# Seven products in the second phase of a feed-forward network, and products that collect on PSUM banks

## The chip, the cores and the metric

The kernel runs on one core of one Trainium2 chip. The metric is the device time of one execution in microseconds. Lower is better.

## What is computed

The reference is one layer of a streaming encoder over 1024 prompt frames and 64 sample frames (T = 1088 tokens) of width 1024. Two feed-forward networks stand around an attention and a convolution branch. The change touches the two feed-forward networks alone:

```
def _swiglu(x, g, w_in, w_out):
    a, b = jnp.split(_rms(x, g) @ w_in, 2, axis=-1)
    return (jax.nn.silu(a) * b) @ w_out

h = x + 0.5 * _swiglu(x, ffn1_norm, ffn1_w_in, ffn1_w_out)
...
h = h + 0.5 * _swiglu(h, ffn2_norm, ffn2_w_in, ffn2_w_out)
```

`w_in` is 1024 x 5632 and `w_out` is 2816 x 1024. The 2816 features are 22 tiles of 128. All values are fp32.

## The kernel before

**Precision.** Each fp32 operand is split into two parts in the type fp32r: `hi` is a copy on ACT, `lo = x - hi` a subtraction on DVE or POOL (`split`, lines 148 to 152). A product of two operands is three matmuls, hi x hi, hi x lo and lo x hi (`mm3`, lines 133 to 137), all into the same PSUM bank.

**Tokens and calls.** h lies in SBUF with channels on the partitions: 8 channel tiles by 1088 tokens, in four token quarters of `HW` = 272. `ffn` is called four times: for each of the two networks once for each half of the tokens (s = 0 or 1), and a half is two quarters c = 0 and 1. A call goes through its 22 feature tiles in groups (`GROUPS`, sizes 4, 4, 4, 3, 3, 4). Each group has a phase 1, which makes the group's features g, and a phase 2, which multiplies g by the group's rows of `w_out` and adds half of the result to h.

**Phase 1** (`wops`, `product`, `up`) makes one feature tile for both quarters. Its gate and linear columns, two halves of the channels and two token quarters form a 2 x 2 by 2 x 2 block product, which Strassen's method (in Winograd's form) computes with seven block products instead of eight. `prep` makes the seven operands of the tokens once for a call (`xop`). `wops` loads the two weight blocks of the tile (512 KB each, issued on SP's queue into `raw`) and makes the seven operands of the weights: `halves` splits the first block as it is, four sums `s` are formed on DVE, and `put` splits them and the block b1 into tiles `wp`. Sums 0 and 2 lie in PSUM banks, 1 and 3 in SBUF tiles. A product is 4 x 3 = 12 matmuls. Each of the seven goes to a fresh PSUM bank, and `up` adds it on DVE to sums held in SBUF (`spare`, `u3`). Silu and multiplication follow, and a split of g into `gh` and `gl`.

**Phase 2** (`part`, `ph2`) is a plain product. For each of the 16 pairs (dm, c) of a channel tile and a quarter, the G feature tiles of the group are accumulated on one bank, G x 3 matmuls, and line 427 adds half of the bank to h on DVE. Weights come in four blocks of two channel tiles, each split as a whole (`wload`, ACT then POOL). The first `NOPEN` = 3 pairs are opened with G - 1 tiles each, so that PE has work while the last tile of phase 1 is finished.

**Order of the work.** The program is written for a tile framework that puts the instructions of each engine in one static order, by a simulated timeline and by priorities; `high_priority(n)` moves a block's instructions n places ahead. `WAHEAD` = 4000 is that of all weight loading and preparation. Each engine runs its instructions in that order. Buffers are few: eight PSUM banks for everything in these stages, three `raw` buffers (`NRAW`), six `wp` tiles (`NPART`), four `s` tiles, three pairs `whi`, `wlo`, and four pairs `gh`, `gl`. A buffer's next writer waits for its last reader. Normalisation of other tokens (`stats`, `prep`, `apply`) is put between, one step after each feature tile and one after every second pair of phase 2, from the generator `steps`; in the last group of a call the function `tail` does so.

In the first call, the first two products of three feature tiles in each of the first two groups (`LEAD`) are computed ahead, while the second quarter of the tokens is being normalised.

Of the kernel before, what the change touches and what calls it, by code (L numbers as in the profile page):

```python
# [9 lines left out]
F32 = mybir.dt.float32  # L10
F32R = mybir.dt.float32r
# [4 lines left out]
AF = mybir.ActivationFunctionType  # L16
ALU = mybir.AluOpType
AX = mybir.AxisListType

P = 128  # L20
D = 1024
KT = 8
# [7 lines left out]
HW = 272  # L30
GROUPS = [4, 4, 4, 3, 3, 4]
LEAD = (3, 3)
NRAW = 3
AHEAD, LAG = 2, 2
# [57 lines left out]
class Kern:  # L92
# [40 lines left out]
    def mm3(self, out, wh, wl, xh, xl, first, last):  # L133
        t = self.nc.tensor
        t.matmul(out, wh, xh, start=first, stop=False)  # L135
        t.matmul(out, wh, xl, start=False, stop=False)  # L136
        t.matmul(out, wl, xh, start=False, stop=last)  # L137
# [151 lines left out]
    def wops(self, offs, a11=True):  # L289

        nc = self.nc
        res = [None] * 7
        with self.tc.high_priority(WAHEAD):
            ra, rb = (self.wraw.tile([P, 1024], F32, name="raw", tag="raw") for _ in range(2))
            for t, o in ((ra, offs[0]), (rb, offs[1])):
                nc.sync.dma_start(t, self.a["wf"][o:o + P * 1024].rearrange("(p n) -> p n", p=P))
            if a11:
                res[0], res[1] = self.halves(ra)
            a0, a1, b0, b1 = ra[:, 0:512], ra[:, 512:1024], rb[:, 0:512], rb[:, 512:1024]
            s = [self.wsum.tile([P, 512], F32, name="s", tag="s") if i % 2 else self.psum() for i in range(4)]  # L300
# [6 lines left out]
            nc.vector.tensor_tensor(s[0], b0, b1, op=ALU.add)  # L307
            nc.vector.tensor_tensor(s[1], s[0], a0, op=ALU.subtract)
            put(2, s[1])
            put(4, s[0])  # L310
            nc.vector.tensor_tensor(s[2], a0, b0, op=ALU.subtract)
            put(3, s[2])
            nc.vector.tensor_tensor(s[3], a1, s[1], op=ALU.subtract)
# [26 lines left out]
    def up(self, w, gp, tp, lead=None):  # L340
        nc = self.nc
        v = nc.vector.tensor_tensor
        self.turn ^= 4
        p1, sa, u2, c22 = (self.spare[:, self.turn + i, :] for i in range(4))
        u3 = tp.tile([P, HW], F32, name="u3", tag="u3", bufs=2)
        if lead:
            p1, sa = lead
        else:
            self.up1(w[0], w[1], p1, sa)
        v(u2, p1, self.product(w[2], 2), op=ALU.add)  # L350
        v(u3, u2, self.product(w[3], 3), op=ALU.add)
        p5 = self.product(w[4], 4)
        v(u2, u2, p5, op=ALU.add)
        v(c22, u3, p5, op=ALU.add)
        g = gp.tile([P, 2 * HW], F32R, name="gh", tag="gh"), gp.tile([P, 2 * HW], F32R, name="gl", tag="gl")
        c = self.product(w[5], 5)
        v(c, u3, c, op=ALU.add)
        v(c, sa, c, op=ALU.mult)
        self.split(g[0][:, :HW], g[1][:, :HW], c)
        c = self.product(w[6], 6)  # L360
        v(c, u2, c, op=ALU.add)
        nc.scalar.activation(c, c, AF.Silu)
        v(c, c22, c, op=ALU.mult)
        self.split(g[0][:, HW:], g[1][:, HW:], c)
        return g

    def ffn_offs(self):
        return [([(self.woff(), self.woff()) for _ in range(G)], [self.woff(2 * G * P) for _ in range(4)])
                for G in GROUPS]

    def ffn(self, h, s, offs, gp, tp, steps, tail, lead=(), ready=(), last=False, lp=None):
# [4 lines left out]
        for gi, n in enumerate(lead):  # L376
            for j in range(n):
# [5 lines left out]
                t = lp.tile([P, 2 * HW], F32, name="gl", tag="gl") if gi else \  # L383
                    gp.tile([P, 2 * HW], F32, name="gf", tag="gh")
                early[gi, j] = t[:, :HW], t[:, HW:]
                self.up1(*w, *early[gi, j])
                next(steps, None)
        if lead:
            run(ready)
        for gi, (wi, wo) in enumerate(offs):  # L390
            G = len(wi)
            gs = []
            for j in range(G):
                e = early.get((gi, j))
                gs.append(self.up(self.wops(wi[j], e is None), gp, tp, e))
                next(steps, None)
            per = 2
            wu = {}

            def part(dm, c, p, js):  # L400
                wh, wl = wu[dm // per]
                b = slice(c * HW, c * HW + HW)
                for j in js:
                    o = ((dm % per) * G + j) * P
                    self.mm3(p, wh[:, o:o + P], wl[:, o:o + P], gs[j][0][:, b], gs[j][1][:, b], j == 0, j == G - 1)

            def ph2(tiles, n, then):

                ps = {}
                for i, (dm, c) in enumerate(tiles):  # L410
                    if dm // per not in wu:
                        wu[dm // per] = self.wload(wo[dm // per], per * G * P)
                    if i < n:
                        if i == 0:
                            for q in tiles[:n]:
                                if q[0] // per not in wu:
                                    wu[q[0] // per] = self.wload(wo[q[0] // per], per * G * P)
# [12 lines left out]
            if gi < len(offs) - 1 or not last:  # L430
                ph2([(dm, c) for dm in range(KT) for c in (0, 1)], NOPEN,
                    (lambda dm, c: c and next(steps, None)) if gi < len(offs) - 1 else tail)
# [6 lines left out]
    def run(self):  # L439
        tc, nc, a = self.tc, self.nc, self.a  # L440
        PS = bass.MemoryType.PSUM
        with ExitStack() as top:
# [59 lines left out]
            gp = self.pool(ffw, "gp1", 4)  # L502
# [880 lines left out]
            gp = self.pool(top, "gp2", 4, side="right")  # L1383
# [45 lines left out]
def _pack_ffn(out, w1, w2):  # L1429
    j0 = 0  # L1430
    for G in GROUPS:
# [3 lines left out]
        for u in range(4):  # L1435
            blk = w2[j0 * P:(j0 + G) * P, u * 2 * P:(u + 1) * 2 * P].reshape(G, P, 2, P)
            out.append(blk.transpose(1, 2, 0, 3).ravel())
# [107 lines left out]
```

## Time and profile before

| | |
|---|---|
| median of three runs | 2393.53 us (2390.45 to 2393.75) |
| the profiled execution | 2389.32 us, span 2387.5 us |
| PE busy | 2291.5 us, 96%, 16610 matmuls |
| DVE busy | 1658.5 us, 69% |
| POOL busy | 1418.2 us, 59% |
| ACT busy | 1197.3 us, 50% |
| granted clock of PE, mean | 0.984 |
| DMA | 273.42 MB, mean 115 GB/s |

PE is TensorE, DVE VectorE, ACT ScalarE, POOL GpSimd, SP SyncE. In a row of a group of instructions stand the line, the engine, the operation, out<-in by the program's names, the shapes, the count, then the busy time in us and the mean of one in ns, and then the idle time of the engine just before them with what ended it. Matmuls are pipelined, so the mean of one is longer than the distance from one to the next. In a row of the waits view stand the waiting engine and line, what it waited for, the sum in us, how often, and the longest.

### The profile page before, as it was taken

Reading aid. Unit: us, or ns where it says so; the run is one execution under the profiler, and the core shown is the slowest. Engines: PE = TensorE matmul, PEld = TensorE weight load, DVE = VectorE, ACT = ScalarE, POOL = GpSimd, SP = SyncE. Lnnn points to the kernel's source line nnn. Section 1 sums busy time; section 2 is a strip of 40 time slices with the busy share of each in tenths; the row PEclk is TensorE's granted clock in tenths of the full one; section 3 lists DMA queues with packets and bytes.
Section 4 is the critical chain, followed back from the end, with each engine's and each line's share of the span. In section 5 each row is a group of like instructions: output and inputs, shape, how many; then the busy total and the mean of one; then the engine's idle time right before and its main releaser. Section 6 shows DMA issues by size and latency. Waiting matters only on the chain. (4 is left out here: it accounts for less than half of the span.)

```text
span 2387.5 us, 43966 instructions
## 1 busy us (share of the span) xinstructions
PE 2291.5 (96%) x16610; PEld 2262.8 (95%) x16610; DVE 1658.5 (69%) x3722; ACT 1197.3 (50%) x2286; POOL 1418.2 (59%) x879
## 2 busy tenths in 40 slices
PE   6999999999999999999979899899999999999998
PEld 6999999999999999999979789799999999999997
DVE  7766677767668387689846777358766678676666
ACT  6343444434345546887556667445433445434343
POOL 5455555555557786888953555467455555455554
PEclk9999999999999999999989999999999999999999
DMA  5323233233223344234222455763222331332223
GB/s 193 106 96 103 92 98 109 99 106 105 82 98 122 129 146 120 90 106 128 95 83 76 141 165 180 222 197 127 79 98 90 106 101 65 119 108 98 89 98 117
DMA packets 130406, 273.42 MB, mean 115 GB/s; under 512 B 17936, under 2 KB 77200, under 8 KB 130192
## 3 DMA queue, kind: packets, MB, share of 16 engines
q1 hardware_dynamic: 130192, 270.61, 35.1%
q8 instruction: 130, 2.13, 0.4%
q14 instruction: 84, 0.69, 0.1%
HBM read 231.87 MB, written 38.75 MB: 113 GB/s over the span
## 5 line engine op out<-in xcount | busy, mean ns | idle before, releaser
L118 POOL TENSOR_TENSOR wlo<-raw,whi 128x1024 fp32r<-128x1024 f32 (+1 forms) x187 | 433.8, 2325 | 356.1 <-ACT whi L117 345.3
L135 PE MATMUL ps<-x,wp 128*128 128x272 f32 x1760 | 506.9, 290 | 2.9 <-ACT wp L151 2.9
L137 PE MATMUL ps<-x,wp 128*128 128x272 f32 x1760 | 504.2, 290 | 1.4 <-DVE wp L152 1.0
L136 PE MATMUL ps<-x,wp 128*128 128x272 f32 x1760 | 505.3, 288 | 0.0
L135 PE MATMUL ps<-x,whi 128*128 128x272 f32 (+2 forms) x1544 | 482.5, 313 | 9.8 <-DVE sg L622 3.2
L137 PE MATMUL ps<-x,wlo 128*128 128x272 f32 (+2 forms) x1544 | 481.2, 312 | 0.0
L136 PE MATMUL ps<-x,whi 128*128 128x272 f32 (+2 forms) x1334 | 412.3, 309 | 0.9 <-POOL x L152 0.9
L135 PE MATMUL ps<-gh,whi 128*128 128x272 f32 x1408 | 400.6, 290 | 5.6 <-DVE spare L283 3.9
L136 PE MATMUL ps<-gl,whi 128*128 128x272 f32 x1408 | 405.6, 290 | 0.0
L137 PE MATMUL ps<-gh,wlo 128*128 128x272 f32 x1408 | 404.6, 289 | 0.0
L152 POOL TENSOR_TENSOR wlo<-raw,whi 128x1024 fp32r<-128x1024 f32 x88 | 220.1, 2502 | 259.3 <-ACT whi L151 248.3
L135 PEld LDWEIGHTS ps<-x,wp 128*128 128x128 f32 x1760 | 331.7, 188 | 4.0 <-ACT wp L151 3.8
L137 PEld LDWEIGHTS ps<-x,wp 128*128 128x128 f32 x1760 | 329.2, 188 | 3.1 <-DVE wp L152 2.5
L136 PEld LDWEIGHTS ps<-x,wp 128*128 128x128 f32 x1760 | 332.0, 189 | 0.0
L152 POOL TENSOR_TENSOR wp<-s,wp 128x512 fp32r<-128x512 f32 x176 | 256.5, 1457 | 98.1 <-ACT wp L151 98.1
L135 PEld LDWEIGHTS ps<-x,whi 128*128 128x128 f32 x1544 | 293.0, 190 | 12.2 <-DVE sg L622 3.5
L117 ACT ACTIVATE whi<-raw 128x1024 fp32r<-128x1024 f32 (+1 forms) x187 | 190.3, 1019 | 211.7 <-DMA raw<-wf 97.2
L137 PEld LDWEIGHTS ps<-x,wlo 128*128 128x128 f32 x1544 | 292.9, 190 | 1.3
L427 DVE SCALAR_TENSOR_TENSOR h<-ps,h 128x272 f32<-128x272 f32 x384 | 164.9, 439 | 185.7 <-PE ps L137 185.0
L679 POOL TENSOR_TENSOR ac<-ac,pd 128x559 f32<-128x559 f32 x180 | 270.5, 1503 | 39.2 <-ACT pd L678 13.7
L135 PEld LDWEIGHTS ps<-gh,whi 128*128 128x128 f32 x1408 | 263.7, 189 | 7.2 <-DVE spare L283 4.5
L137 PEld LDWEIGHTS ps<-gh,wlo 128*128 128x128 f32 x1408 | 266.6, 190 | 0.0
(254 smaller groups left out, 4818.6 us busy)
## 6 DMA issues: line engine op xcount, KB each, us to landing
raw<-wf SPq DMA_DIRECT2D x337, 512.0 KB, 3.4
raw<-wf SPq DMA_DIRECT2D x32, 384.0 KB, 3.2
d_g<-sg SPq DMA_DIRECT2D x32, 181.0 KB, 1.9
d_h<-h SPq DMA_DIRECT2D x2, 2176.0 KB, 10.7
y<-t SPq DMA_DIRECT2D x32, 136.0 KB, 1.9
raw<-d_q SPq DMA_DIRECT2D x32, 128.0 KB, 3.5
raw<-d_qi SPq DMA_DIRECT2D x24, 128.0 KB, 3.1
d_g<-sg SPq DMA_DIRECT2D x16, 182.0 KB, 3.3
```

The source lines that it names most:

```text
L117: nc.scalar.activation(hi[:, :n], raw[:, :n], AF.Copy)
L118: self.weng.tensor_tensor(lo[:, :n], raw[:, :n], hi[:, :n], op=ALU.subtract)
L135: t.matmul(out, wh, xh, start=first, stop=False)
L136: t.matmul(out, wh, xl, start=False, stop=False)
L137: t.matmul(out, wl, xh, start=False, stop=last)
L152: (eng or nc.vector).tensor_tensor(lo, x, hi, op=ALU.subtract)
L427: nc.vector.scalar_tensor_tensor(x, p, 0.5, x, op0=ALU.mult, op1=ALU.add)
L679: nc.gpsimd.tensor_tensor(ac, ac, pd, op=ALU.add)
```

## The change

Five things change together.

- `GROUPS` becomes 4, 4, 4, 4, 2, 4.
- Phase 2 of a group of four that is not the last of its call (`down`) also becomes a 2 x 2 by 2 x 2 block product with seven products: over the even and the odd tile of a pair of feature tiles, the lower and the upper half of the channels, and two token quarters. `up` makes the seven operands of g for a pair (t1 to t4 are their sums), in tiles of seven planes. `wops` makes those of the weights. `down` is called twice for a group (u = 0 and 1), each time for two channel tiles (i) of each half. Groups of two and the last group keep the plain phase 2, with the weights packed in another order.
- Products collect on banks. In `up`, products 2 and 3 are accumulated onto the bank of product 0, product 6 onto that of 4, and 5 onto that of 0, 2 and 3; between them `keep` copies the bank's state to SBUF on ACT, at priority `CHI` = 8000, or DVE reads it. In `down`, the banks "a" (products 0, 2, 3, 5) and "d" (4, 6) work alike, and after each product DVE adds the bank to the quarter and half of h that it belongs to; product 1 has bank "b".
- The order of the products becomes 0, 4, 2, 1, 3, 6, 5.
- In `wops`, ACT first copies b0 to a PSUM bank, so that three of the four sums have one operand there. With `sb` (in `down`), the other three sums lie in SBUF, and POOL makes every `lo` but that of sum 0, which DVE makes. `halves` copies its block in two pieces.

The core of the diff (the code that makes the weights' packing and the plain phase 2 is left out):

```diff
-GROUPS = [4, 4, 4, 3, 3, 4]
+GROUPS = [4, 4, 4, 4, 2, 4]
+CHI = 8000
...
-    def wops(self, offs, a11=True):
+    def wops(self, offs, a11=True, sb=False):
 
         nc = self.nc
         res = [None] * 7
+        v = nc.vector.tensor_tensor
         with self.tc.high_priority(WAHEAD):
             ra, rb = (self.wraw.tile([P, 1024], F32, name="raw", tag="raw") for _ in range(2))
             for t, o in ((ra, offs[0]), (rb, offs[1])):
@@ -297,38 +299,47 @@
             if a11:
                 res[0], res[1] = self.halves(ra)
             a0, a1, b0, b1 = ra[:, 0:512], ra[:, 512:1024], rb[:, 0:512], rb[:, 512:1024]
-            s = [self.wsum.tile([P, 512], F32, name="s", tag="s") if i % 2 else self.psum() for i in range(4)]
-
-            def put(o, x):
+            s = [self.wsum.tile([P, 512], F32, name="s", tag="s") if i % 2 or (sb and i) else self.psum()
+                 for i in range(4)]
+
+            def put(o, x, eng=None):
                 t = self.wpart.tile([P, 1024], F32R, name="wp", tag="wp")
                 res[o] = t[:, 0:512], t[:, 512:1024]
-                self.split(*res[o], x, nc.vector if o in (3, 4) else self.weng)
-
-            nc.vector.tensor_tensor(s[0], b0, b1, op=ALU.add)
-            nc.vector.tensor_tensor(s[1], s[0], a0, op=ALU.subtract)
+                self.split(*res[o], x, eng or self.weng)
+
+            nc.scalar.activation(s[0], b0, AF.Copy)
+            v(s[2], a0, s[0], op=ALU.subtract)
+            v(s[0], s[0], b1, op=ALU.add)
+            put(4, s[0], nc.vector)
+            v(s[1], s[0], a0, op=ALU.subtract)
             put(2, s[1])
-            put(4, s[0])
-            nc.vector.tensor_tensor(s[2], a0, b0, op=ALU.subtract)
-            put(3, s[2])
-            nc.vector.tensor_tensor(s[3], a1, s[1], op=ALU.subtract)
+            put(3, s[2], None if sb else nc.vector)
+            v(s[3], a1, s[1], op=ALU.subtract)
+            put(6, s[3])
             put(5, b1)
-            put(6, s[3])
         return res
 
     def halves(self, raw):
         hi = self.wsp.tile([P, 1024], F32R, name="whi", tag="whi")
         lo = self.wsp.tile([P, 1024], F32R, name="wlo", tag="wlo")
-        self.split(hi, lo, raw, self.weng)
+        for c in (slice(0, 512), slice(512, 1024)):
+            self.nc.scalar.activation(hi[:, c], raw[:, c], AF.Copy)
+        self.weng.tensor_tensor(lo, raw, hi, op=ALU.subtract)
         return (hi[:, 0:512], lo[:, 0:512]), (hi[:, 512:1024], lo[:, 512:1024])
 
-    def product(self, wop, o):
-        out = self.psum()[:, :HW]
+    def product(self, wop, o, onto=None):
+        out = self.psum()[:, :HW] if onto is None else onto
         xh, xl = self.xop(o)
         wh, wl = wop
         for k in range(4):
             c = slice(k * P, k * P + P)
-            self.mm3(out, wh[:, c], wl[:, c], xh[:, k, :], xl[:, k, :], k == 0, k == 3)
+            self.mm3(out, wh[:, c], wl[:, c], xh[:, k, :], xl[:, k, :], onto is None and k == 0, k == 3,
+                     onto is not None)
         return out
+
+    def keep(self, out, x):
+        with self.tc.high_priority(CHI):
+            self.nc.scalar.activation(out, x, AF.Copy)
 
...
+    def up(self, w, tp, g, odd, seven, lead=None):
+        act = nc.scalar.activation
+        p1, sa, u2, p5 = (self.spare[:, self.turn + i, :] for i in range(4))
+        t1, g12 = sa, u2
+        c22 = tp.tile([P, HW], F32, name="u3", tag="u3", bufs=2)
         if lead:
             p1, sa = lead
+            d = self.product(w[4], 4)
+            self.keep(p5, d)
+            v(u2, p1, self.product(w[2], 2), op=ALU.add)
+            self.product(w[6], 6, d)
+            c = self.product(w[3], 3)
+            v(c, u2, c, op=ALU.add)
+            v(c22, c, p5, op=ALU.add)
+            b = self.product(w[5], 5)
+            self.keep(p5, c)
+            v(c, p5, b, op=ALU.add)
         else:
+            c = self.product(w[0], 0)
+            self.keep(p1, c)
+            d = self.product(w[4], 4)
+            self.keep(p5, d)
+            self.product(w[2], 2, c)
+            self.keep(u2, c)
+            v(sa, p1, self.product(w[1], 1), op=ALU.add)
+            act(sa, sa, AF.Silu)
+            self.product(w[3], 3, c)
+            v(c22, c, p5, op=ALU.add)
+            self.product(w[6], 6, d)
+            self.product(w[5], 5, c)
+        v(d, u2, d, op=ALU.add)
+        act(d, d, AF.Silu)
+        put = lambda o, x, eng=None: self.split(g[0][:, o, :], g[1][:, o, :], x, eng)
+        if not seven:
+            v(d, c22, d, op=ALU.mult)
+            v(c, sa, c, op=ALU.mult)
+            put(2 * odd + 1, d)
+            put(2 * odd, c)
+        elif not odd:
+            v(g12, c22, d, op=ALU.mult)
+            v(c, sa, c, op=ALU.mult)
+            put(0, c)
+            v(t1, g12, c, op=ALU.subtract)
+            put(4, t1, nc.gpsimd)
+            self.held = t1, g12
+        else:
+            t1, g12 = self.held
+            t2, t3, t4 = (tp.tile([P, HW], F32, name="t", tag="t") for _ in range(3))
+            v(d, c22, d, op=ALU.mult)
+            v(t2, d, t1, op=ALU.subtract)
+            put(2, t2)
+            v(c, sa, c, op=ALU.mult)
+            put(1, c)
+            put(6, d)
+            v(t3, d, g12, op=ALU.subtract)
+            put(3, t3, nc.gpsimd)
+            v(t4, c, t2, op=ALU.subtract)
+            put(5, t4, nc.gpsimd)
...
+    def down(self, h, s, wo, gs, u, then):
+
+        nc = self.nc
+        w = self.wops((wo[2 * u], wo[2 * u + 1]), sb=True)
+        banks = {}
+        todo = [(dm, c) for dm in range(4 * u, 4 * u + 4) for c in (0, 1)]
+        plan = ((0, "a", ((0, 0),)), (4, "d", ((1, 1),)), (2, "a", ((0, 1),)), (1, "b", ((0, 0),)),
+                (3, "a", ((1, 1),)), (6, "d", ((0, 1),)), (5, "a", ((1, 0),)))
+        for o, bank, outs in plan:
+            for i in range(2):
+                onto = (bank, i) in banks
+                if not onto:
+                    banks[bank, i] = self.psum()[:, :HW]
+                p = banks[bank, i]
+                for q, (gh, gl) in enumerate(gs):
+                    wh, wl = w[o]
+                    b = slice((2 * q + i) * P, (2 * q + i) * P + P)
+                    self.mm3(p, wh[:, b], wl[:, b], gh[:, o, :], gl[:, o, :], not onto and q == 0,
+                             q == len(gs) - 1, onto)
+                for half, c in outs:
+                    t0 = (2 * s + c) * HW
+                    x = h[:, 4 * half + 2 * u + i, t0:t0 + HW]
+                    nc.vector.scalar_tensor_tensor(x, p, 0.5, x, op0=ALU.mult, op1=ALU.add)
+            then(*todo.pop(0))
+        then(*todo.pop(0))
+
...
+            end = gi == len(offs) - 1
+            seven = G == 4 and not end
+            hook = (lambda dm, c: c and next(steps, None)) if not end else tail
             gs = []
             for j in range(G):
+                if j % 2 == 0:
+                    gs.append(tuple(gp.tile([P, 7, HW], F32R, name=n, tag=n) for n in ("gh", "gl")))
                 e = early.get((gi, j))
-                gs.append(self.up(self.wops(wi[j], e is None), gp, tp, e))
+                self.up(self.wops(wi[j], e is None), tp, gs[-1], j % 2, seven, e)
                 next(steps, None)
-            per = 2
+            if seven:
+                for u in range(2):
+                    self.down(h, s, wo, gs, u, hook)
+                continue
             wu = {}
```

More of the change, by code (lines that the diff above doesn't have):

```diff
@@ L130, in woff, with mm3 @@
         return o
-    def mm3(self, out, wh, wl, xh, xl, first, last):
+    def mm3(self, out, wh, wl, xh, xl, first, last, onto=False):
         t = self.nc.tensor
-        t.matmul(out, wh, xh, start=first, stop=False)
-        t.matmul(out, wh, xl, start=False, stop=False)
-        t.matmul(out, wl, xh, start=False, stop=last)
+        t.matmul(out, wh, xh, start=first, stop=False, skip_group_check=onto)
+        t.matmul(out, wh, xl, start=False, stop=False, skip_group_check=onto)
+        t.matmul(out, wl, xh, start=False, stop=last, skip_group_check=onto)
     def proj(self, out, wt, xh, xl, nk, o0=0):
@@ L346, in up @@
         if lead:
             p1, sa = lead
-        else:
[L349 to L365, printed above, removed]
+            d = self.product(w[4], 4)
[4 more added lines that the diff above has]
+            v(c, u2, c, op=ALU.add)
@@ L376, in ffn @@
         for gi, n in enumerate(lead):
+            if gi == 0:
+                first = gp.tile([P, 7, HW], F32, name="gf", tag="gh")
             for j in range(n):
@@ L382, in ffn @@
                     w = self.halves(ra)
-                t = lp.tile([P, 2 * HW], F32, name="gl", tag="gl") if gi else \
-                    gp.tile([P, 2 * HW], F32, name="gf", tag="gh")
-                early[gi, j] = t[:, :HW], t[:, HW:]
+                if gi:
+                    t = lp.tile([P, 2 * HW], F32, name="gl", tag="gl")
+                    early[gi, j] = t[:, :HW], t[:, HW:]
+                else:
+                    early[gi, j] = first[:, 2 * j, :], first[:, 2 * j + 1, :]
                 self.up1(*w, *early[gi, j])
@@ L391, in ffn, with load @@
             G = len(wi)
+            end = gi == len(offs) - 1
+            seven = G == 4 and not end
+            hook = (lambda dm, c: c and next(steps, None)) if not end else tail
             gs = []
             for j in range(G):
+                if j % 2 == 0:
+                    gs.append(tuple(gp.tile([P, 7, HW], F32R, name=n, tag=n) for n in ("gh", "gl")))
                 e = early.get((gi, j))
[L395 removed]
+                self.up(self.wops(wi[j], e is None), tp, gs[-1], j % 2, seven, e)
                 next(steps, None)
[L397 removed]
+            if seven:
+                for u in range(2):
+                    self.down(h, s, wo, gs, u, hook)
+                continue
             wu = {}
+            unit = lambda dm: (dm // 4) + 2 * (dm % 4 // 2)
+            def load(dm):
+                if unit(dm) not in wu:
+                    wu[unit(dm)] = self.wload(wo[unit(dm)], 2 * G * P)
             def part(dm, c, p, js):
[L401 to L402 removed]
+                wh, wl = wu[unit(dm)]
                 for j in js:
[L404 to L405 removed]
+                    o = ((j % 2 * (G // 2) + j // 2) * 2 + dm % 2) * P
+                    gh, gl = gs[j // 2]
+                    b = j % 2 * 2 + c
+                    self.mm3(p, wh[:, o:o + P], wl[:, o:o + P], gh[:, b, :], gl[:, b, :], j == 0, j == G - 1)
             def ph2(tiles, n, then):
@@ L410, in ph2 @@
                 for i, (dm, c) in enumerate(tiles):
-                    if dm // per not in wu:
-                        wu[dm // per] = self.wload(wo[dm // per], per * G * P)
+                    load(dm)
                     if i < n:
@@ L415, in ph2 @@
                             for q in tiles[:n]:
-                                if q[0] // per not in wu:
-                                    wu[q[0] // per] = self.wload(wo[q[0] // per], per * G * P)
+                                load(q[0])
                                 ps[q] = self.psum()[:, :HW]
@@ L428, in ph2 @@
                     then(dm, c)
-            if gi < len(offs) - 1 or not last:
-                ph2([(dm, c) for dm in range(KT) for c in (0, 1)], NOPEN,
-                    (lambda dm, c: c and next(steps, None)) if gi < len(offs) - 1 else tail)
+            if not (end and last):
+                ph2([(dm, c) for dm in range(KT) for c in (0, 1)], NOPEN, hook)
             else:
@@ L1382, in run @@
             self.wpart = self.pool(top, "wpart2", NPART, side="right")
-            gp = self.pool(top, "gp2", 4, side="right")
+            gp = self.pool(top, "gp2", 2, side="right")
             offs = self.ffn_offs()
@@ L1434, in _pack_ffn @@
             out.append(_unit(w1[:, FF + j * P:FF + (j + 1) * P]))
-        for u in range(4):
-            blk = w2[j0 * P:(j0 + G) * P, u * 2 * P:(u + 1) * 2 * P].reshape(G, P, 2, P)
-            out.append(blk.transpose(1, 2, 0, 3).ravel())
+        for m in (0, 4, 2, 6):
+            blk = w2[j0 * P:(j0 + G) * P, m * P:(m + 2) * P].reshape(G // 2, 2, P, 2, P)
+            out.append(blk.transpose(2, 1, 0, 3, 4).ravel())
         j0 += G
```

5 lines of the change are left out of this document (1 added, 4 removed).

## The prediction

> **What bounds the kernel now.** I read the page's busy table and its forty slices first, to see which engine is the limit and where.
>
> ```profile
> PE 2291.5 (96%) x16610; PEld 2262.8 (95%) x16610; DVE 1658.5 (69%) x3722; ACT 1197.3 (50%) x2286; POOL 1418.2 (59%) x879
> PE   6999999999999999999979899899999999999998
> PEclk9999999999999999999989999999999999999999
> ```
>
> TensorE is busy in nearly every slice, at its full granted clock. The two feed-forward stages (slices 1 to 13 and 28 to 40) show nines throughout. So time there is the number of matmuls times the pace of one. The windows view gives the pace: a whole stretch, then one phase 2 and one phase 1 of a group of four feature tiles.
>
> ```profile
> 240.00:300.00 60.00, 60.00 (x479) 60.00 (x478) 41.46 (x84) 25.25 (x48) 34.92 (x20) 1.00 0.29 93
> 2180.50:2204.50 24.00, 24.00 (x193) 24.00 (x193) 11.40 (x23) 4.36 (x6) 7.85 (x4) 1.00 0.18 61
> 2205.20:2247.20 42.00, 42.00 (x335) 42.00 (x335) 28.19 (x58) 18.08 (x36) 22.32 (x14) 1.00 0.33 105
> ```
>
> Columns are busy time and count of PE, PE's weight loads, DVE, ACT and POOL, then clock and DMA. 479 matmuls in 60 us are 125.3 ns each (the 290 ns in the groups below overlap). Phase 2 (192 matmuls by the code) takes 24 us, phase 1 of four tiles (4 x 84 = 336) takes 42 us, at the same pace. PE has no gap in any of the three; DVE is at 67% in phase 1 and 48% in phase 2. The groups of instructions give the prices of what the change moves.
>
> ```profile
> L135 PE MATMUL ps<-x,wp 128*128 128x272 f32 x1760 | 506.9, 290 | 2.9 <-ACT wp L151 2.9
> L135 PE MATMUL ps<-gh,whi 128*128 128x272 f32 x1408 | 400.6, 290 | 5.6 <-DVE spare L283 3.9 <-DVE h L427 1.0 <-DVE x L152 0.7
> L118 POOL TENSOR_TENSOR wlo<-raw,whi 128x1024 fp32r<-128x1024 f32 x155 | 374.4, 2421 | 251.8 <-ACT whi L117 243.6 <-PE lg L1099 6.4 <-PE ps L136 0.9
> L152 POOL TENSOR_TENSOR wp<-s,wp 128x512 fp32r<-128x512 f32 x176 | 256.5, 1457 | 98.1 <-ACT wp L151 98.1
> L152 POOL TENSOR_TENSOR wlo<-raw,whi 128x1024 fp32r<-128x1024 f32 x88 | 220.1, 2502 | 259.3 <-ACT whi L151 248.3 <-PE ps L137 11.0
> L427 DVE SCALAR_TENSOR_TENSOR h<-ps,h 128x272 f32<-128x272 f32 x384 | 164.9, 439 | 185.7 <-PE ps L137 185.0
> L117 ACT ACTIVATE whi<-raw 128x1024 fp32r<-128x1024 f32 x155 | 163.3, 1055 | 153.3 <-DMA raw<-wf 69.6 <-PE ps L136 57.1 <-issue 16.6
> L152 POOL TENSOR_TENSOR wp<-raw,wp 128x512 fp32r<-128x512 f32 x88 | 114.7, 1303 | 2.7 <-ACT wp L151 1.5
> L152 DVE TENSOR_TENSOR wp<-ps,wp 128x512 fp32r<-128x512 f32 x176 | 114.5, 680 | 0.2
> L151 ACT ACTIVATE wp<-s 128x512 fp32r<-128x512 f32 x176 | 111.1, 631 | 204.5 <-DVE s L308 188.3 <-DVE s L313 13.2 <-PE ps L137 1.9
> L313 DVE TENSOR_TENSOR s<-raw,s 128x512 f32<-128x512 f32 x88 | 100.7, 1145 | 0.1
> L311 DVE TENSOR_TENSOR ps<-raw 128x512 f32<-128x512 f32 x88 | 94.5, 1074 | 0.0
> L307 DVE TENSOR_TENSOR ps<-raw 128x512 f32<-128x512 f32 x88 | 83.9, 954 | 2.5 <-DMA raw<-wf 2.4
> L308 DVE TENSOR_TENSOR s<-ps,raw 128x512 f32<-128x512 f32 x88 | 60.0, 682 | 0.0
> L151 ACT ACTIVATE gh<-ps 128x272 fp32r<-128x272 f32 x176 | 69.3, 395 | 121.2 <-DVE ps L358 90.1 <-DVE ps L363 30.6
> L152 POOL TENSOR_TENSOR x<-spare,x 128x272 fp32r<-128x272 f32 x32 | 25.9, 814 | 20.8 <-ACT x L151 20.0 <-PE ps L136 0.4
> ```
>
> I take 0.44 us for every 272-wide DVE operation (L427), 0.40 for ACT, 0.81 for POOL. The matmul rows hardly wait (2.9 and 5.6 us): PE's operands are ready long before it needs them.
>
> **The change part by part.**
>
> *Phase 2, matmuls.* A group of four (not the last of a call) now needs 2 calls of `down` x 7 products x 2 channel tiles x 2 pairs x 3 = 168 matmuls instead of 16 x 4 x 3 = 192. Four such groups in each of four calls make 16 groups, so 384 fewer. Going from sizes 3 and 3 to 4 and 2 changes nothing by itself: 144 + 144 matmuls become 192 + 96, and the 192 is among the sixteen. Gain: 384 x 125.3 ns = 48.1 us.
>
> *Phase 2, weights.* Four plain loads per group (ACT 4 x 1.06 = 4.2 us, POOL 4 x 2.42 = 9.7, DVE 0) become two sets of seven operands. One set costs ACT a copy, two halves and five splits, 8 x 0.63 = 5.0; POOL 2.50 + 3 x 1.46 + 1.30 = 8.2; DVE three sums with one PSUM operand, one with two SBUF operands and one split, 3 x 0.68 + 1.15 + 0.68 = 3.9. DMA bytes and transfers stay the same: four 512 KB blocks per group either way. SP passes no queue that it did not pass before.
>
> *Phase 2, adds into h.* 14 per `down` instead of 8, each 0.44: 6.2 us. So each `down`, 10.5 us on PE, asks DVE for 10.1, POOL for 8.2, ACT for 5.0. The durations overlap: phase 1's window shows 28.2 us busy where the same sum over four tiles (3.86 + 2 x 0.68 + 11 x 0.44 = 10.1 each) says 40. True demand is about 7 of 10.5 us, so DVE has room on average.
>
> *Phase 1.* Products 2 and 3 go onto product 0's bank, 6 onto 4's, 5 onto 3's, so four DVE adds go and two ACT copies (`keep`) come. Each weight set loses two of its three SBUF-with-SBUF subtractions on DVE (0.95 + 1.07 become 0.68 + 0.68) for one ACT copy of 0.63 and 0.2 more for halves in two pieces. The pair sums t1 to t4 and three more splits per pair in seven-product groups bring DVE from 22 to 18 operations, ACT from 10 to 17 (2.8 us more) and POOL from 0 to 3 (2.4 us more) in PE's 21 us. All three stay below PE on average, so I cost these at nothing; if POOL lost its cover, weight lows would be late next.
>
> *From phase 1 to phase 2.* Planes 0 and 4 of both pairs come from the even tiles, so 24 matmuls (3.0 us) cover the last tile's chain, where `NOPEN` gave 27 before (3.4 us). I cost it at nothing; if a sum is caught behind a POOL operation of 2.4 us, up to 1 us x 16.
>
> *The new waits.* This is the unknown. Before, products went to fresh banks and a late reader cost PE nothing. Now PE may not add product 2 before ACT has copied product 0, nor product 3 before the second copy, nor product 5 before DVE has made c22; in `down`, PE waits three times for the adds into h. Behind a held matmul everything on PE's queue waits. One product is 12 x 125.3 ns = 1.5 us. From the last row's end (290 ns after its start) to the next use of its bank PE leaves 1.34 us in `up`, and 0.44 of it is the reader's own: 0.9 us to spare. In `down`, with 18 matmuls between, 1.65. How late are readers now? The waits view, the source view of two sums, and the timeline:
>
> ```profile
> ACT wp L151 <- DVE s L308: 188.3, 78, 6.3
> DVE h L427 <- PE ps L137: 185.0, 222, 1.5
> DVE u L351 <- PE ps L137: 47.8, 55, 1.5
> L307 DVE TENSOR_TENSOR ps<-raw x88: 689/693/2610, 41.4 to 2332.7; 128x512 f32<-128x512 f32 x88
> L308 DVE TENSOR_TENSOR s<-ps,raw x88: 675/682/689, 43.8 to 2333.9; 128x512 f32<-128x512 f32 x88
> 2223.18 0.29 PE L137 MATMUL ps<-x,wp 128*128 128x272 f32 x1
> 2222.35 2.24 DVE L307 TENSOR_TENSOR ps<-raw 128x512 f32<-128x512 f32 x1
> 2224.51 0.69 DVE L311 TENSOR_TENSOR ps<-raw 128x512 f32<-128x512 f32 x1
> 2225.11 0.68 DVE L308 TENSOR_TENSOR s<-ps,raw 128x512 f32<-128x512 f32 x1
> 2225.71 0.42 DVE L353 TENSOR_TENSOR spare<-spare,ps 128x272 f32<-128x272 f32 x1
> ```
>
> The PE row is the last matmul of product 4. Its result stands at 2223.47, but its reader L353 starts 2.24 us later, behind a burst of weight sums. Under the new rules PE would have stood 1.3 us. Of 88 readers of product 3 (L351), 55 found DVE waiting for them and 33 came late. The burst shortens to 3 x 0.68 + 1.15 = 3.2 us. If it fell anywhere in a tile's 10.5 us, the loss would be (3.2 - 0.9)^2 / (2 x 10.5) = 0.25 us a tile, 20 us over the 82 tiles without a head start. At the other end, it falls between the new readers of DVE, and the loss is 0. In `down` the same sum is 3 x (3.2 - 1.65)^2 / 21 = 0.34 us, 11 us over 32 calls; other end 0, which is nearer to the 222 of 384 L427 that found DVE idle. For the copies on ACT: in these groups no operation there is longer than 0.63 once the halves are cut, so only ACT standing at the head of its queue costs. It did so for L308 78 times, 188.3 / 78 = 2.4 us each: (2.4 - 0.9)^2 / 21 = 0.11 per copy, two copies, 82 tiles, 18 us; other end 0, and the copies' priority and the shorter burst put it there. I take 10 + 5 + 3 = 18 us between ends 0 and 49.
>
> *The sum.* The profiled execution took 2389.3 us. 2389.3 - 48.1 + 18 = 2359.2. The median of the three runs shown, 2393.5, is 4.2 us above it, so on that scale 2363.
>
> **The rivals.**
>
> *All readers are in time.* For it: the sums that took up to 2610 ns (L307) now have a PSUM operand, like L308, which never exceeded 689. Against it: a burst of several 0.68 remains. 2389.3 - 48.1 + 4.2 = 2345; with up to 8 us of stalls, 2353.
>
> *The waits eat the gain, and more.* The mechanism is one: in each tile a weight burst stands in DVE's queue ahead of c22 (or an add into h), held by its last subtraction a1 - s1, which has two SBUF operands as L307 had and runs beside a POOL that has more to do. If every unit repeats the 1.3 us of the timeline's example in half of the cases, that is 0.65 x (88 + 32) = 78 us: 2389.3 - 48.1 + 78 + 4.2 = 2423. It decides at 48.1 / 120 = 0.40 us lost per seven products: below that the change is faster, above it slower. For it: the scheduler puts weight work 4000 places ahead and c22 not at all, and L353's burst sits just where c22 will. Against: 55 of 88 and 222 of 384 prompt readers, and an earlier burst when fewer sums precede it. The Trainium skill, "SBUF — State Buffer", section "Who interferes with whom", says that a DVE instruction with two SBUF inputs and a GpSimd instruction that reads SBUF exclude each other for a whole instruction. The rows agree: 2610 ns at most for L307, 689 for L308 with a PSUM operand; by that rule the two sums replaced stop stalling, a1 - s1 does not.
>
> *No change that can be measured.* The upper ends together: 49 us lost against 48.1 gained, 2394.
>
> *The products are not fewer in time.* If matmuls that reuse a bank ran slower than 125.3 ns, the gain would go without a wait; the accumulating rows now (L135 on gh, 290 ns) stand like all others, so I give it no chance of its own.
>
> **How the numbers follow.** Measurement tells about 0.2%, 4.8 us, from no change. Chances: readers in time (2345 to 2353) 0.22; part of the gain lost (2353 to 2376, likeliest 2363) 0.36; most of it lost (2376 to 2388.7) 0.14; within 0.2% 0.07; slower 0.21. Faster is 0.22 + 0.36 + 0.14 = 0.72. The range runs from 2342, a little under the full gain, to 2402, which takes in the no-change case and the near part of the slower one and leaves out 0.02 below and 0.17 above. The likeliest case's own range is 2353 to 2376.
>
> **What would show it.** 16226 matmuls instead of 16610, still 125 ns apart in full stretches; a phase 2 of 21 us in place of 24. PE's idle before the first row of a product (L135's successors, released by ACT `keep` or DVE c22 or the add into h) gives the lost time: near 18 us if I am right, near 0 or over 48 if a rival is. The sums after the ACT copy should stay under 0.7 us, a1 - s1 should not. I am wrong if PE waits instead for weight operands (a POOL or ACT split late in `down`), for planes 1 to 3 at the phase boundary, or for a bank held by another tile.

## The result, and the profile after

The changed kernel takes 2367.4 us (median of four runs) against 2393.6 us: a ratio of 0.989, interval 0.9875 to 0.9905. The profiled executions took 2364.2 and 2389.3 us, 25.1 us apart. (A few single executions, of either kernel, took up to 2.5 times as long; no time here includes them, and the only profile of experiment 10 is one of them.) PE has exactly 384 matmuls fewer. The page's busy table after:

```profile
PE 2254.3 (95%) x16226; PEld 2216.6 (94%) x16226; DVE 1690.9 (72%) x3868; ACT 1416.6 (60%) x2926; POOL 1557.9 (66%) x1071
```

DVE has 32 us more work, POOL 140, ACT 219. The pace has not changed. This is the windows view after, over a stretch with phase 1 and seven-product phase 2:

```profile
480.00:540.00 60.00, 60.00 (x480) 60.00 (x479) 48.62 (x107) 34.69 (x76) 41.86 (x30) 1.00 0.29 92
```

480 matmuls in 60 us, as before. To see what became of 48.1 us, the windows view is asked for the four feed-forward calls, each from its first to its last matmul. First before, then after; the columns are the window, its length, then busy time and count of PE, PE's weight loads, DVE, ACT and POOL, clock and DMA. (The counts hold some other matmuls, those of the norms.)

```profile
17.50:407.38 389.88, 377.24 (x2933) 374.22 (x2934) 279.37 (x605) 172.25 (x346) 216.78 (x137) 0.99 0.31 100
407.50:781.13 373.63, 371.05 (x2941) 369.50 (x2940) 262.65 (x561) 164.15 (x321) 216.23 (x127) 1.00 0.32 107
1628.47:2002.82 374.35, 371.12 (x2928) 369.94 (x2928) 263.64 (x558) 162.47 (x317) 210.70 (x126) 1.00 0.28 94
2002.95:2373.36 370.41, 369.93 (x2941) 369.53 (x2940) 256.03 (x551) 155.10 (x296) 204.51 (x114) 1.00 0.31 104
sum 1508.27, PE 1489.34 PEld 1483.18 DVE 1061.68 ACT 653.97 POOL 848.20; mean PE 372.33 PEld 370.80 DVE 265.42 ACT 163.49 POOL 212.05
```

```profile
17.41:397.61 380.20, 368.96 (x2838) 361.91 (x2838) 292.30 (x656) 227.06 (x506) 252.28 (x185) 1.00 0.31 102
397.74:764.88 367.14, 361.07 (x2845) 357.72 (x2844) 268.00 (x592) 218.95 (x477) 250.41 (x175) 1.00 0.34 110
1616.43:1982.04 365.61, 360.12 (x2832) 357.49 (x2832) 267.76 (x588) 217.13 (x476) 245.03 (x174) 1.00 0.30 96
1982.17:2348.43 366.26, 360.88 (x2846) 357.53 (x2844) 264.33 (x582) 209.44 (x452) 238.89 (x162) 1.00 0.33 105
sum 1479.21, PE 1451.02 PEld 1434.64 DVE 1092.39 ACT 872.58 POOL 986.61; mean PE 362.76 PEld 358.66 DVE 273.10 ACT 218.15 POOL 246.65
```

A call has 2904 matmuls before and 2808 after; at 125.3 ns each from start to start they need 4 x 2903 x 0.1253 = 1455.0 and 4 x 2807 x 0.1253 = 1406.9 us. What the sums have above that I call lost time: 53.3 us before, 72.3 after. (About 16 us of both are no loss but the matmuls of the norms, 127 before and 129 after.) So the calls gained 48.1 - 19.0 = 29.1 us. The stretch between the two networks, whose code is unchanged, went from 847.3 us (781.13 to 1628.47) to 851.6 (764.88 to 1616.43), 4.2 us more; start and end together are 0.2 us shorter. The sum is 48.1 - 19.0 - 4.2 + 0.2 = 25.1 us.

For whom PE waited is seen best where it loads weights, since the load before a matmul meets the wait first (c22 after: 0.8 us at the load, 0.5 at the matmul). These are the rows of the waits view for that queue, before and then after, that belong to weight operands (`wp`), to the readers of banks (before, L427 is the add into h; after, L342 is the copy in `keep`, L439 the add into h, L381 c22) and, after, to the planes of g (`gh`):

```profile
PEld ps L135 <- ACT wp L151: 3.8, 4, 1.4
PEld ps L137 <- DVE wp L152: 2.5, 6, 0.8
PEld ps L137 <- POOL wp L152: 0.4, 1, 0.4
PEld ps L135 <- DVE h L427: 1.2, 2, 0.6
```

```profile
PEld ps L136 <- ACT wp L152: 5.4, 9, 2.0
PEld ps L138 <- DVE wp L153: 4.4, 12, 0.6
PEld ps L136 <- ACT spare L342: 4.4, 9, 0.8
PEld ps L138 <- POOL wp L153: 4.2, 6, 1.1
PEld ps L136 <- ACT gh L152: 3.5, 5, 1.2
PEld ps L136 <- DVE h L439: 3.5, 7, 0.9
PEld ps L136 <- DVE u L381: 0.8, 1, 0.8
```

Readers hold PE 8.7 us instead of 1.2, weight operands 14.0 instead of 6.7, planes 3.5 instead of nothing that the view lists. Together that is 18.3 us more, close to the 19.0 that the calls lost. No single wait of these rows is longer than 2.0 us. The weight sums, in the source view after (least, median and greatest ns of one):

```profile
L311 DVE TENSOR_TENSOR ps<-raw,ps x88: 679/695/697, 40.6 to 2303.7; 128x512 f32<-128x512 f32 x88
L312 DVE TENSOR_TENSOR ps<-ps,raw x120: 686/693/693, 41.2 to 2304.3; 128x512 f32<-128x512 f32 x120
L317 DVE TENSOR_TENSOR s<-raw,s x120: 676/685/2868, 44.8 to 2307.7; 128x512 f32<-128x512 f32 x120
```

The two sums that now have a PSUM operand never exceed 697 ns. The one that keeps two SBUF operands still reaches 2868.

### The profile page after: what moved, and what is told of

Its sections match the earlier page's. It is cut to its first block, busy times and chain, and to the rows that moved or that the text cites. A ratio compares the mean times of both kernels' runs of the same rounds, so it can differ in the third digit from the quotient of the medians.

```text
span 2362.4 us, 44344 instructions
## 1 busy us (share of the span) xinstructions
PE 2254.3 (95%) x16226; PEld 2216.6 (94%) x16226; DVE 1690.9 (72%) x3868; ACT 1416.6 (60%) x2926; POOL 1557.9 (66%) x1071
## 5 line engine op out<-in xcount | busy, mean ns | idle before, releaser
L153 POOL TENSOR_TENSOR wp<-s,wp 128x512 fp32r<-128x512 f32 x272 | 363.9, 1349 | 190.0 <-ACT wp L152 185.9
L327 POOL TENSOR_TENSOR wlo<-raw,whi 128x1024 fp32r<-128x1024 f32 x120 | 290.4, 2420 | 186.7 <-ACT whi L326 177.8
L119 POOL TENSOR_TENSOR wlo<-raw,whi 128x1024 fp32r<-128x1024 f32 (+1 forms) x123 | 277.9, 2262 | 154.0 <-ACT whi L118 149.1
L136 PEld LDWEIGHTS ps<-x,whi 128*128 128x128 f32 x1544 | 292.8, 190 | 13.4 <-ACT sg L1138 3.9
L137 PEld LDWEIGHTS ps<-x,whi 128*128 128x128 f32 x1334 | 253.6, 190 | 2.3 <-POOL x L153 1.3
L152 ACT ACTIVATE wp<-s 128x512 fp32r<-128x512 f32 x272 | 167.8, 626 | 130.3 <-DVE s L314 80.6
L765 ACT ACTIVATE pd<-ci,par 128x559 f32<-128x559 f32 x180 | 135.7, 758 | 96.8 <-POOL ac L766 85.8
L152 ACT ACTIVATE wp<-ps 128x512 fp32r<-128x512 f32 x208 | 123.1, 592 | 113.1 <-DVE ps L312 100.2
L439 DVE SCALAR_TENSOR_TENSOR h<-ps,h 128x272 f32<-128x272 f32 x448 | 174.9, 431 | 13.1 <-PE ps L138 12.4
L326 ACT ACTIVATE whi<-raw 128x512 fp32r<-128x512 f32 x240 | 138.5, 624 | 74.5 <-DMA raw<-wf 70.4
L137 PE MATMUL ps<-gl,whi 128*128 128x272 f32 x640 | 182.7, 291 | 0.0
```

The lines of the kernel that those rows point to most:

```text
L119: self.weng.tensor_tensor(lo[:, :n], raw[:, :n], hi[:, :n], op=ALU.subtract)
L136: t.matmul(out, wh, xh, start=first, stop=False, skip_group_check=onto)
L137: t.matmul(out, wh, xl, start=False, stop=False, skip_group_check=onto)
L152: nc.scalar.activation(hi, x, AF.Copy)
L153: (eng or nc.vector).tensor_tensor(lo, x, hi, op=ALU.subtract)
L326: self.nc.scalar.activation(hi[:, c], raw[:, c], AF.Copy)
```

## The experiments

Each ratio is to the kernel before as it was measured beside the experiment, with medians of 2388.1 to 2390.9 us there against 2393.6 beside the change, so ratios compare better than times. Whole times hold the unchanged middle stretch too. It took 847.3, 851.6 and 854.2 us in experiment 1, the change and experiment 4, where PE's matmuls stand in one and the same order there, and 860.3 and 863.5 in experiments 2 and 3, where they stand in another. Where a kernel's values differ, it moves with the values. So each experiment is read by the lost time of its four calls, worked out as above.

**1. Collecting in phase 1 alone.**

```diff
-            seven = G == 4 and not end
+            seven = False
```

> The changed kernel with the plain phase 2 in every group (the seven-product `down` is never called), the collecting `up` and the new weight sums kept. The four feed-forward calls have 11616 matmuls again, as before the change. Theory A (the gain is only the 384 matmuls, and the new waits in both phases cost something): 2393.6 plus what collecting in `up` costs. After the change the rows of phase 1 lost 14 us more than before, so about 2400 (2394 to 2408). Theory B (PE waits because weight preparation in `down` is late and pushes phase 1 back): without `down` phase 1 loses nothing more, 2393 or a little under. Theory C (collecting relieves DVE and helps by itself): under 2389.

Measured: 2397.3 us, ratio 1.003 (1.0017 to 1.0043). Its four calls:

```profile
sum 1511.09, PE 1489.32 PEld 1478.12 DVE 875.44 ACT 767.74 POOL 816.93; mean PE 372.33 PEld 369.53 DVE 218.86 ACT 191.93 POOL 204.23
```

Lost: 1511.1 - 1455.0 = 56.1 us, 3 above the kernel before. So collecting costs PE next to nothing. Together with the new weight sums, which this kernel keeps, it takes 186 us off DVE (1062 to 875); 82 us of that are the sums' (279.1 us for L307, L311 and L313 before, 197.1 for L311, L312 and L317 here). By itself it gains nothing, because PE is the bound. The 14 us that the expectation put on phase 1 appear only with `down` present.

**2. Seven products in phase 2 without collecting in phase 1.** In `up`, for tiles without a head start:

```diff
-            self.product(w[2], 2, c)
-            self.keep(u2, c)
+            v(u2, p1, self.product(w[2], 2), op=ALU.add)
...
-            self.product(w[3], 3, c)
-            v(c22, c, p5, op=ALU.add)
-            self.product(w[6], 6, d)
-            self.product(w[5], 5, c)
+            v(u3, u2, self.product(w[3], 3), op=ALU.add)
+            v(u2, u2, p5, op=ALU.add)
+            v(c22, u3, p5, op=ALU.add)
+            d = self.product(w[6], 6)
+            c = self.product(w[5], 5)
+            v(c, u3, c, op=ALU.add)
```

> The changed kernel, but in `up` (tiles without a head start) every product goes to a bank of its own and DVE makes the sums in SBUF, as before the change, in the new order of products; `down` still collects. No copy `keep` and no c22 holds PE in those tiles; DVE has four operations of 0.44 us more per tile. Theory A (bank readers in `up` cost 4 to 5 us now: 3.9 by the copies, 0.7 by c22): 2363, or the same if DVE's work makes something else late. The prediction's split (13 us by these readers): 2354. Theory D (DVE would be too full without collecting): 2375 or more, with PE waiting for weight operands that DVE splits.

Measured: 2404.8 us, ratio 1.0055 (1.0036 to 1.0074): slower than before the change. The calls, and the waits of PE's weight loads:

```profile
sum 1511.26, PE 1466.89 PEld 1438.79 DVE 1222.07 ACT 824.58 POOL 997.83; mean PE 366.72 PEld 359.70 DVE 305.52 ACT 206.14 POOL 249.46
```

```profile
PEld ps L136 <- ACT wp L152: 17.3, 29, 1.7
PEld ps L137 <- DVE gl L153: 8.3, 13, 1.7
PEld ps L136 <- DVE h L439: 7.4, 18, 1.9
PEld ps L138 <- DVE wp L153: 6.7, 16, 1.3
PEld ps L138 <- POOL wp L153: 6.2, 14, 1.2
```

Lost: 1511.3 - 1406.9 = 104.4 us. With 130 us more on DVE, the waits for weight operands double (14.0 to 30.2) and those for the adds into h too. So the 384 matmuls gain nothing without collecting in phase 1: it makes the room on DVE that `down` uses. (The middle stretch is 860.3 us here, in another static order, and adds 9 us more.)

**3. The copies without priority.** `keep` without its `high_priority(CHI)`.

> The changed kernel with `keep` at ordinary priority, so that weight work 4000 places ahead goes before the copies on ACT. Theory A with the prediction's upper end for these copies (18 us against 3.9 now): about 2380, with PE's waits for the copies (L342 or its successor line) at 10 us or more. If ACT has room enough that the order does not matter: 2367, with these waits still near 4 us.

Measured: 2379.0 us, ratio 0.9939 (0.9919 to 0.996). It looks like the 12 us that were expected, but is not. The calls:

```profile
sum 1484.18, PE 1450.14 PEld 1433.06 DVE 1095.48 ACT 873.82 POOL 988.13; mean PE 362.54 PEld 358.26 DVE 273.87 ACT 218.46 POOL 247.03
```

Lost: 77.3 us, 5 more than with priority, and PE's loads wait 5.5 us for the copies instead of 4.4. The rest is the middle stretch, 863.5 us against 851.6. PE's matmuls stand there in the same static order as in experiment 2, in which 1160 of the 4838 places hold another matmul than in the changed kernel. In one profile each, the priority is worth some 5 us; the upper end that I gave these copies, 18 us, is far off.

**4. Readers first.** c22 and the adds into h at priority 8000, like the copies.

> The changed kernel with DVE's readers of collecting banks (c22 in `up`, the adds into h in `down`) at the priority of the copies, 8000, so that they go before weight sums. Prediction's mechanism (bursts of weight sums ahead of readers, 15 us): 2355 or less. Theory A (these readers cost 3.1 + 0.7 = 3.8 us now): at best 2363.5. Theory B (weight operands are the scarcer thing, and they come later if readers go first): 2367 to 2372, with more time lost at operands wp.

Measured: 2365.7 us, ratio 0.9885 (0.9867 to 0.9904), not to be told from the change; lost 71.5 us (1478.36 - 1406.9). PE's loads still wait for the same readers, 0.8 us for c22 and, for the adds, no less than the 3.5 of the change:

```profile
PEld ps L136 <- DVE h L441: 5.7, 7, 1.4
```

So an earlier place in DVE's order does not shorten what is left of these waits.

**5. The weight sums from SBUF again.**

```diff
-            nc.scalar.activation(s[0], b0, AF.Copy)
-            v(s[2], a0, s[0], op=ALU.subtract)
-            v(s[0], s[0], b1, op=ALU.add)
+            v(s[2], a0, b0, op=ALU.subtract)
+            v(s[0], b0, b1, op=ALU.add)
```

> The changed kernel with the first two weight sums as before the change: b0 + b1 and a0 - b0 with both operands in SBUF, no copy of b0 on ACT (0.60 us less there per tile or `down`). In the rows of before such sums took 0.95 and 1.07 us on average and up to 2.9, beside POOL's subtractions; with one PSUM operand 0.68. Theory D (DVE is the scarce engine once `down` is there, so each us on it in these stages is felt): about 0.65 us more per unit, 120 units, 78 us more DVE time, of which PE feels a good part: 2385 or more. If DVE has room: 2367, or a little less because ACT is relieved.

Measured: 2479.3 us, ratio 1.0369 (1.0342 to 1.0396), 112 us slower than the change. The calls; the two sums by the source view (L310 in phase 1, L311 in both); and PE's waits (L380 is c22, L438 the add into h, L341 the copy):

```profile
sum 1588.22, PE 1487.95 PEld 1456.16 DVE 1250.04 ACT 807.45 POOL 1046.72; mean PE 371.99 PEld 364.04 DVE 312.51 ACT 201.86 POOL 261.68
```

```profile
L310 DVE TENSOR_TENSOR ps<-raw x88: 690/1116/4797, 39.6 to 2422.9; 128x512 f32<-128x512 f32 x88
L311 DVE TENSOR_TENSOR ps<-raw x120: 680/1536/2897, 40.8 to 2424.2; 128x512 f32<-128x512 f32 x120
```

```profile
PEld ps L136 <- DVE u L380: 34.9, 19, 4.1
PEld ps L136 <- DVE h L438: 23.1, 24, 2.3
PEld ps L136 <- ACT spare L341: 21.1, 20, 2.3
```

Lost: 181.3 us, 109 more. The readers of banks hold PE 79 us instead of 8.7: the prediction's slower rival, a burst of weight sums ahead of a reader. DVE's work grew by 158 us, but the amount alone does not tell, since experiment 2, with 1222 us of DVE, had no such readers in most tiles of phase 1. The timeline does. This is one of the 19 waits for c22; its bank was complete at 184.45, and PE's load stood for 2.2 us until c22 (L380) had read it:

```profile
184.88 2.56 DVE L310 TENSOR_TENSOR ps<-raw 128x512 f32<-128x512 f32 x1 [2.40 <-DMA raw<-wf]
187.35 1.75 DVE L311 TENSOR_TENSOR ps<-raw 128x512 f32<-128x512 f32 x1
189.01 0.43 DVE L380 TENSOR_TENSOR u<-ps,spare 128x272 f32<-128x272 f32 x1
```

In all 19, weight sums with two SBUF operands ran between the bank's last matmul and c22, for 1.9 to 4.1 us against 0.9 to spare, 55 of 81 us in sum; for another 21 us DVE stood idle there, mostly at the head of its queue until the weight block had landed. (That part belongs to the order of DVE's work, which is another here, not to the length of the sums.) The copies on ACT come late by the same sums: ACT's splits of them waited 293 us for L311, and 100 us for the sum in that place of the change. With one copy of 0.60 us on ACT, little of this is left. The Trainium skill, "SBUF — State Buffer", section "Who interferes with whom", says that a DVE instruction with two SBUF inputs and a GpSimd instruction that reads SBUF shut each other out for a whole instruction. The trace agrees: all 184 sums of L310 and L311 that took over 0.75 us ran beside a POOL instruction, while in the change 201 of the 240 sums of L311 and L312 ran beside one too and, with a PSUM operand, none took over 697 ns.

**6. More tiles for weight operands.** Eight `wp` tiles instead of six in the second network.

> The changed kernel with eight `wp` tiles instead of six in the second feed-forward network only (the first has no room). Theory E (PE waits for weight operands because their tiles come free too late): the second network's two calls, which lost 13.9 and 14.5 us, lose 8 or 9 each as before the change, the first's stay at 28.5 and 15.4; about 2356. Theory D (DVE) or a late POOL: the second network's calls keep 28 us, 2367.

Measured: 2375.7 us, ratio 0.9935 (0.9912 to 0.9958): slower than the change (0.989), not faster. The calls sum to 1491.02 us, lost 84.1. The second network's two calls took 369.81 and 370.94 us instead of 365.61 and 366.26, and there lost 9 us more. So more tiles do not bring the time back. Why it is slower was not pursued.

**7. Narrow adds.** The adds into h over 16 of 272 columns; the rest of the result is left out.

> The changed kernel with the 14 adds into h in each `down` cut to 16 of 272 columns: all waits between PE and DVE stay, but each add is about 0.25 us shorter, 3.5 us of DVE per `down` and 112 us in all. Left out: the other columns of the result. Theory D (DVE is the scarce engine): the time lost in the four calls falls from 72 us towards the 56 us of the kernel with the plain phase 2, about 2352. Theory E or a late POOL: it stays near 72, 2364 to 2367.

**8. Fewer low parts.** In `down`, operands 5 and 6 without the subtraction on POOL; their high part stands in for the low part.

> The changed kernel with POOL relieved in `down`: the low parts of weight operands 5 and 6 are not made (left out: their high part is used in their place, so matmuls stay the same in number). POOL has 1.30 + 1.35 us less per `down`, 85 us in all. Theory F (POOL's splits come late because phase 2 now asks 8.2 of its 10.5 us): lost time falls from 72 towards 56, about 2352, and PE's waits for POOL's wp vanish. Theory D: no change, 2367.

Measured, the calls of 7 and of 8:

```profile
sum 1475.83, PE 1448.75 PEld 1434.62 DVE 987.43 ACT 874.54 POOL 984.99; mean PE 362.19 PEld 358.65 DVE 246.86 ACT 218.63 POOL 246.25
```

```profile
sum 1483.43, PE 1452.68 PEld 1435.10 DVE 1087.04 ACT 873.87 POOL 910.71; mean PE 363.17 PEld 358.78 DVE 271.76 ACT 218.47 POOL 227.68
```

DVE has 105 us less in the one and loses 69.0 us, 3 less than the change; POOL has 76 us less in the other and loses 76.6. So at the change's level less work of these kinds on either engine brings PE nothing clear, although 130 us more on DVE (experiment 2) is felt at once. The whole times, 2350.4 and 2510.0 us, say nothing here: the altered values pass through the selection of keys (in 8 DVE ran 4282 instructions instead of 3868), and the middle stretch took 841.4 and 989.9 us.

**9. Group sizes alone,** on the kernel before.

> The kernel before with the new group sizes alone (4, 4, 4, 4, 2, 4). The same 11616 matmuls in the four calls. The prediction costed it at nothing: lost time in the four calls stays near 53 us, the time within 0.2% of before. Rival: the group of two lets PE wait for its weight blocks, four of 256 KB in 12 us: 5 to 10 us slower.

Measured: 2388.8 us, ratio 1.0 (0.9988 to 1.0012); the calls sum to 1506.84 us, lost 51.9. Nothing, as costed.

**10. The changed kernel again.**

> The changed kernel once more, unaltered, for a second profile: how far the time lost in the four calls (72.3 us) and the stretch between the two networks (851.6 us, 847.3 before) move between executions of one program. If the 4.2 us more in that stretch are chance, it comes out anywhere from 847 to 855; if they belong to the changed order there, again near 851.6. Lost time near 72, and its split over readers, weight operands and planes similar.

Measured: 2363.7 us, ratio 0.9888 (0.9865 to 0.9912), on another chip than experiments 1 to 8. Its profile is not used, so how lost time moves between executions stays open. The only hint is what the kernel before and experiment 9 differ by, 53.3 and 51.9 us; differences of 5 us between single profiles are to be read with that in mind.

**11. Seven products also in the last group of each network's first call** (`seven = G == 4 and not (end and last)`), **and 12. five such groups in each call** (`GROUPS = [4, 4, 4, 4, 4, 2]`).

> The changed kernel with the seven-product phase 2 also in the last group of the first call of each network, where the other half's tokens are prepared at the same time: 48 matmuls fewer, 6.0 us. DVE is busy 23.96 of 26.00 us there now, so theory D (DVE is the scarce engine wherever it is full) says the gain is lost and more: 2368 to 2378. If only order matters: 2361.

> The changed kernel with sizes 4, 4, 4, 4, 4, 2: five groups of a call with the seven-product phase 2 instead of four, 96 matmuls fewer in all, 12.0 us. The last phase 2 of a call, under which the next tokens are prepared or the last rows normalised, is 12 us instead of 24. If that work is not exposed: 2355. If it is (the last phase 2 already loses 23 us in the four calls together, and its cover is halved): up to 12 us more per call, 2370 to 2400.

Measured: 2375.6 us, ratio 0.9934 (0.9914 to 0.9953), and 2396.2 us, ratio 1.002 (1.0003 to 1.0037). Both have fewer matmuls than the change and are slower. In 11 the first call of each network loses; this is the end of the first:

```profile
384.00:409.00 25.00, 17.62 (x107) 16.82 (x106) 23.23 (x58) 12.45 (x31) 11.40 (x12) 0.80 0.13 43
```

DVE is busy 23.2 of 25 us, since the other half's tokens are prepared there; PE only 17.6, and its granted clock is 0.80. Of 8.1 us that PE's loads wait there, 5.2 are for operands that DVE makes and 2.9 for one of ACT. The call lost 43 us instead of 28. In 12 the calls sum to 1511.27 us for 11136 matmuls (1394.8 us): lost 116.4. Much of that lies at the ends of the calls too: in the last 25 or 26 us of the four, PE is busy 77.4 of 102 us, against 92.3 in the change. So the last phase 2 of a call, under which other tokens are prepared, is where fewer matmuls do not pay; that a full DVE is the reason is borne out by these rows for 11 only. In 12's last call DVE is busy 16.8 of the last 25 us, and PE waits 6.0 us there for the sums of a norm. No kernel that makes the whole result beats the change clearly.

## Why the prediction was right, point by point

- *Gain by fewer matmuls, 48.1 us:* right. 16226 matmuls at the same pace.
- *Lost to new waits, 18 us:* the calls lost 19.0 us more. The size was right, the split was not, so the size is in part luck. I put 10 us on c22, 5 on the adds into h, 3 on the copies, and nothing on weight operands and planes. PE's loads waited 0.8, 3.5 and 4.4 us for the readers, 7.3 us more than before for weight operands and 3.5 for `gh`. The step that failed is "I cost these at nothing", for the weights and for the planes at the phase boundary: that DVE, ACT and POOL stay below PE on average did not keep their operands in time. The prediction names waits for weight operands and planes as the sign of being wrong, and they are 10.8 of the 18.3 us that were added. The over-sized c22 and the missing weights happened to cancel.
- *c22, the upper end by a burst anywhere in a tile (20 us):* the lower end was nearer. 52 of the 82 c22 found DVE waiting:

```profile
DVE u L381 <- PE ps L138: 65.8, 52, 2.5
```

- *The shorter burst:* right, and worth far more than I took for it. Experiment 5 shows the slower rival's mechanism at 109 us lost, where I had 78; but there the first two sums are the long ones, and DVE's wait for the transfer was not in my account. The sum that I named, a1 - s1, is long in the change as well (L317, up to 2868 ns) and does little harm.
- *Collecting costed as a relief of DVE "at nothing":* wrong in kind. It is what makes the seven products of phase 2 affordable (experiment 2: 32 us more lost without it).
- *Group sizes:* nothing, right (experiment 9).
- *A phase 2 of 21 us in a piece:* not to be seen, because PE's static order mixes products of the last tile and the first `down`. This is the windows view after, narrowed to instructions on `gh`:

```profile
204.50:233.30 28.80, 21.60 (x112) 17.75 (x112) 1.94 (x3) 2.09 (x6) 2.32 (x3) 1.00 0.27 92
```

The 112 rows that read `gh` (two of three of 168) spread over 28.8 us with phase 1 between them. I read that mixing as what hides the chain at the phase boundary now, as the opened tiles did before; no run takes it away.

- *The middle stretch* was not in the sum. 4.2 us of what I missed lie there, and they may be chance: experiment 1, with the same order there, took the 847.3 us of the kernel before.
- *"Nines throughout":* the first and the last slice of PE show 6 and 8. Nothing hangs on it.

What stays open is why `down` adds 16 us of lost time (56.1 in experiment 1, 72.3 in the change). Less work on DVE, less on POOL, more tiles or other priorities did not remove it. Where it lies can be read from the starts of the matmuls, by what each comes later than 125.3 ns after the one ahead of it. Delays of 1 us and more sum to 17.4 us in experiment 1 and 17.6 in the change; shorter ones, above 0.02 us, to 22.7 and 38.3. So it is many short delays. About half of them, 7.3 us, is in the products of phase 1 with `wp` operands (15.5 and 22.8 us, and 7.8 before the change), and 7.2 is in the new products of `down`. The rows of the waits view shown above, taken for both, name 10.4 of the 16 us: 4.8 more for weight operands, 3.5 for the adds into h, 1.1 for planes and 1.0 for the copies. What makes these late, and the rest, stays open.

## What to carry to other kernels

Where one engine is full, fewer of its instructions are worth their number times its pace, less what new waits cost; sum those over all the places where PE can wait, operands included, not only over the waits that the change adds by name. An accumulation onto a bank that another engine must read first has a budget (here 0.9 us): work that stands directly ahead of the reader and takes longer stops the accumulating engine, and here a 0.6 us copy that took one operand of two sums out of SBUF was worth about 100 us. Before explaining a difference of 10 us, split the time by stages: in experiment 3 more than half of it lay in code that nobody touched.

## What the runs showed of the hardware

The subtraction with two SBUF operands lasted up to 4797 ns in experiment 5, twice a POOL subtraction of 2.4 us, although its least was 690 ns; the longest one ran beside five POOL instructions, one after the other. At the end of the first call in experiment 11, with gaps of up to 3.5 us, PE's granted clock was 0.80 over 25 us. In the change, whose longest gap at the end of the third call is 2.1 us, it was 0.93 over the last 26 us of that call.
